# The end of layer 1 of a two-layer recurrent backbone: head 5's output products behind head 7's gates, heads 6 and 7 summed in PSUM, the last norm's squares summed by TensorE

## The chip, the core and the metric

The kernel runs on one core of a Trainium2 chip. The core has TensorE (PE in the profile), which multiplies matrices into PSUM; VectorE (DVE), ScalarE (ACT) and GpSimd (POOL), which work elementwise; and SyncE (SP), which here issues most of the transfers from HBM. Each engine takes its instructions from a queue in the order in which the program was built, and waits in that order. The metric is the time of one execution in microseconds (us), the median of several runs.

## The reference, cut to what matters

A sequence of 256 context tokens and 512 latent tokens (a grid of 8 x 64), 1024 channels wide, goes through two layers. Layer 0 is a gated linear recurrence with 16 heads and is not touched by the change. Layer 1 is this, for each of its 8 heads of 256 channels (all in float32):

```python
xb, g = split(h @ w_in)                      # h: normed and modulated tokens
xb = conv_centred(xb, conv_w, conv_b)        # width 4
r  = sigmoid(xb @ w_a[d] + b_a[d])           # d: two directions
ig = sigmoid(xb @ w_x[d] + b_x[d])
a  = exp(-8 * r * softplus(-lam[d]))
u  = sqrt(1 - a * a) * (ig * xb)
y  = scan(a, u, d=0) + scan(a, u, d=1)       # h[t] = a[t] * h[t-1] + u[t]
x  = x + gate * ((y * silu(g)) @ w_out)      # summed over the heads
out = x * rsqrt(mean(x * x) + eps) * final_norm_g
```

Only the 512 latent tokens are put out.

## The kernel before

**Layout.** Channels lie on the 128 partitions, tokens along the free axis. Each head of layer 1 has two chunks of 128 channels, called `jc`, `e` or `u` (0 and 1). The output has 8 chunks of 128 channels, called `d`. Every product is exact to float32: each operand is split into a high and a low float32r part, and `mm3` issues three matmuls per pair (lines 308, 309, 310: high x high, high x low, low x high).

**Weights.** They come as a stream of [128, 1024] tiles (class `Weights`). Each is loaded by SP into a `raw` tile (line 114); ScalarE copies out the high part `hi` (line 129), VectorE subtracts to get `lo` (line 130). There are three buffers each for `raw`, `hi` and `lo`, so a tile's split waits until the tile three places earlier in the stream has been used up by TensorE.

**A head of layer 1** consists of these parts, named as in the profile:

- `rin`: products of the normed tokens, `r` (PSUM, pool `dps`, four buffers). `x = 0` gives `xb` by the convolution (ScalarE line 758, VectorE line 761), then its two parts `xh` (763) and `xl` (764). `x = 1` gives the output gate `gg` (a sigmoid on ScalarE, line 742, and a product on VectorE, 743).
- `mixer`: the gates. For each of the four keys (direction, chunk), 24 matmuls of 384 columns into four `gt` tiles (PSUM, pool `aps`, four buffers), which ScalarE turns into `R` and `G` by sigmoids (809), and VectorE multiplies `G` by `xb` (811). Then ScalarE takes tanh (818) and two exponentials (820, 821) of each key, then the square roots of all keys (827). VectorE makes `T` (822), the driven input (830), the scans (832 forward; 835 and 836 backward), sum and gate (839, 840); ScalarE and VectorE split the result into `yh` (841) and `yl` (842). Sigmoid, exp and sqrt lie in different function tables of ScalarE, so that each change of kind has an ACT_TABLE_LOAD.
- `rout`: the head's output, 48 matmuls of 512 columns into eight `ro` tiles (`dps`), each added to the residual stream by VectorE (`add_out`, line 848).

`R`, `G` and `T` have four buffers each: a sigmoid of head j + 1 waits until VectorE has scanned the same key of head j.

**Order.** The main loop over the heads runs the mixer as a generator and lets other work be issued between its steps (`interleave`, `phase`): during the gates of head j and during the functions behind them, the products `rin` of head j + 1 and `rout` of head j - 1. For head 6 (`elif not last`) half of head 7's `rin` stands in the first phase and `rout` of head 5 in the second. For head 7 (`else`) the first three keys' gates run with the output-gate half of its own `rin`, the fourth key is a group of its own behind them, and nothing else is between. The program is then scheduled by a framework, which fixes the order on each engine at build time; priorities (`high_priority`, `issue_after`) bend it.

**The end.** `rout(6)` runs whole. Then the products of head 7 with its chunk 0, for all eight `d` over 512 tokens: five are held in PSUM, three are added to the residual at once. Then, for each half of 256 tokens, the products with chunk 1, `add_out`, and `sumsq`: ScalarE squares a chunk (lines 282, 285), and GpSimd and VectorE add the squares into three accumulators (286). `rstd_of` sums the accumulators over the partitions by matmuls of one column (`msf`, line 259), takes the root on ScalarE (262) and its reciprocal (263), and spreads it by `rbf` (269). Sixteen VectorE operations (922) and eight transfers put out the result.

Of the kernel before, what the change touches and what calls it, by code (L numbers as in the profile page):

```python
# [16 lines left out]
NT = CTX + LAT          # tokens, context first  # L17
HN = NT // 2            # token half
ROWS, GW = 8, 64        # latent grid
DK = 8                  # 128-channel chunks of the model width  # L20
NH = 16                 # HGRN2 heads
NC = NT // P            # chunks of 128 tokens
NLEV = 7                # block sizes 1, 2, ... 64 within a chunk
NM = 5                  # of these, the ones within 32 tokens
RH = 8                  # RG-LRU heads
EPS = 1e-6

# the order of the start: a step of adaLN block b (ab), the norm (r), chunk k of h (hk), the weights of the first head's
# product y (wy), their part with chunk k of h (fky), the split of the first value weights (v)
# [3 lines left out]
# columns of the packed parameters  # L33
# [7 lines left out]
# columns of the constants: identity, row selector, 1/1024, 1/128  # L41
# [10 lines left out]
def perm(ap):  # L52
    """latent columns in column-major grid order, walked row by row"""
    return ap.rearrange("p (w r) -> p r w", r=ROWS)
# [6 lines left out]
def phase(main, weight, filler, total):  # L61
    """interleave up to the next None of main, if weight is that of one phase"""
    interleave(upto(main, weight), weight, filler, total)
# [12 lines left out]
class Nothing:  # L76
    """stands in for the program while the order of the weight tiles is taken down"""
# [16 lines left out]
class Weights:  # L94
    """the stream of [128, 1024] weight tiles, loaded ahead and split into two float32r parts"""
# [60 lines left out]
def interleave(main, weight, filler, total):  # L156
    """after each step of main (yields give its weight), its share of the filler (yields give its size)"""
# [11 lines left out]
def build(tc, ins, out, plan):  # L169
# [19 lines left out]
    # ---- constants, small parameters, the residual stream  # L189
# [24 lines left out]
    # silu of both condition vectors, padded to 32 columns  # L214
# [7 lines left out]
    # ---- adaLN: six blocks of 512 columns, four parts of the contraction side by side in the array  # L222
# [28 lines left out]
    # ---- h = rms(x) * g * (1 + scale) + shift, as two float32r parts  # L251
    def rstd_of(accs, ones, tag, parts, between=()):
        """1 / sqrt(mean + eps) of each token from its squares (chunks of 128 tokens; the mean is over the partitions
        and accs), on all partitions: PSUM tiles of so many chunks"""
# [23 lines left out]
    def sumsq(accs, groups, tile_, k, c):  # L278
        """the squares of chunk k of the channels, summed by groups of chunks; the first of three groups on GpSimd"""
# [13 lines left out]
    def hchunk(l, k, i, rs, scr):  # L293
        """chunk k of h for one stretch of tokens; layer 0 keeps the latents in row-major order"""
# [9 lines left out]
    def mm3(ps, pairs, first=True, last=True, skip=False):  # L304
        """exact products of split operands: ps += sum over (whi, wlo, xhi, xlo) of whi xhi + whi xlo + wlo xhi"""
# [9 lines left out]
    # ================= layer 0  # L315
# [98 lines left out]
    def prep(h):  # L414
        """operands of the first two score steps"""
# [9 lines left out]
    def hgrn(h):  # L425
# [4 lines left out]
        # scores [key, query]: same token (both directions), then pairs of neighbouring blocks of 1, 2, ... 64 tokens;  # L430
        # up to 32 tokens the array works on four groups of 32 keys at once
# [49 lines left out]
        # keys with tokens on the partitions (in place), for the chunk states  # L481
# [7 lines left out]
        # states that enter the chunks, in the order of each direction  # L489
# [237 lines left out]
    turn = {}  # L727

    def after(*names):
        """queue ScalarE's instructions behind the last ones of these kinds"""  # L730
        stack = ExitStack()
        for n in names:
            if n in turn:
# [268 lines left out]
```

## Time and profile before

| | |
|---|---|
| median of 3 runs | 1648.79 us (1645.66 to 1650.98) |
| span of the profiled execution, first to last instruction | 1643.9 us |
| median less span, taken as what lies around the span | 4.9 us |
| last stage: first gates of head 6 to the end | 1520.2 to 1643.9 us |
| longest idle time of TensorE after the start | 8.8 us, at 1604.4 |
| busy share over the span | PE 97%, DVE 73%, ACT 52%, POOL 1% |

The page shows the busy share of each engine. A timeline row has the start in the span, the duration, engine, line, operation, what is written and read, how many like instructions were merged, and in brackets how long the engine was idle before it and what ended that. Instructions of one engine overlap a little: on ScalarE the next one starts about 0.1 us before the shown end of the former. Shown ends of matmuls are modelled, so their cost is the distance of their starts.

### The profile page before, as it was taken

How to read it: one execution, taken by the hardware profiler on the slowest of the kernel's cores; microseconds unless marked ns; L12 is line 12 of the kernel's file. 1: busy time of each engine (PE TensorE's matmuls, PEld its weight loads, DVE VectorE, ACT ScalarE, POOL GpSimd, SP SyncE). 2: the span in 40 equal slices, each digit the busy share in tenths (PEclk: the TensorE clock that was granted, in tenths of full speed). 3: DMA queues.
4: the chain of work that ended last, by engine and by line, in shares of the span. 5: the costliest groups of instructions: out<-in, count | busy, mean ns of one | idle time of the engine just before them, and what ended most of it. 6: DMA issues, size and time to landing. Idle time of an engine off the chain costs nothing.

```text
span 1643.9 us, 33639 instructions
## 1 busy us (share of the span) xinstructions
PE 1595.2 (97%) x14548; PEld 1432.9 (87%) x14548; DVE 1203.1 (73%) x1867; ACT 856.0 (52%) x1359; POOL 11.8 (1%) x16
## 2 busy tenths in 40 slices
PE   6999999999999999999999999999999999999995
PEld 3888899999999999898989889888798888888884
DVE  5756668767867777756866675787758977887888
ACT  5544354444443453443444344544567677577774
POOL 0000000000000000000000000001000000000001
PEclk9999999999999999999999999999899999999997
DMA  8222211110211211213031222211022222222211
GB/s 340 65 78 65 91 53 47 58 53 27 75 43 40 66 53 40 82 61 97 33 117 48 82 78 65 89 42 40 26 91 76 74 68 77 74 68 64 78 64 51
DMA packets 33858, 116.76 MB, mean 71 GB/s; under 512 B 3632, under 2 KB 6064, under 8 KB 33712
## 3 DMA queue, kind: packets, MB, share of 16 engines
q1 hardware_dynamic: 32192, 113.26, 21.7%
q8 instruction: 114, 1.87, 0.5%
q10 hardware_dynamic: 1520, 1.37, 0.3%
q14 instruction: 32, 0.26, 0.0%
HBM read 112.52 MB, written 2.10 MB: 70 GB/s over the span
## 4 chain that ended last, share of the span: by engine, by line
PE 88%; DVE 7%; ACT 2%; issue 1%; DMA 1%; POOL 0%; ACTq 0%; POOLq 0%; DVEq 0%
PE in L308 12%; PE in L309 11%; PE in L310 11%; PE v L378 8%; PE ada L228 4%; PE lv L456 4%; PE o L531 3%; PE r L310 3%; PE r L308 3%; PE r L309 3%; PE o L308 3%; PE o L309 3%; PE o L310 2%; PE U L499 2%; PE gt L308 2%; PE gt L309 2%
## 5 line engine op out<-in xcount | busy, mean ns | idle before, releaser
L308 PE MATMUL in<-h_hi,hi 128*128 128x384 f32 x1024 | 355.1, 348 | 1.6 <-ACT h_hi L301 1.6
L309 PE MATMUL in<-h_lo,hi 128*128 128x384 f32 x1024 | 344.7, 337 | 0.4 <-DVE h_lo L302 0.4
L310 PE MATMUL in<-h_hi,lo 128*128 128x384 f32 x1024 | 344.4, 337 | 0.0
L129 ACT ACTIVATE hi<-raw 128x1024 fp32r<-128x1024 f32 x160 | 168.4, 1057 | 195.8 <-PE in L309 106.6
L130 DVE TENSOR_TENSOR lo<-raw,hi 128x1024 fp32r<-128x1024 f32 x160 | 195.0, 1220 | 92.9 <-ACT hi L129 92.8
L308 PEld LDWEIGHTS in<-h_hi,hi 128*128 128x128 f32 x1024 | 192.1, 188 | 35.9 <-issue 27.7
L309 PEld LDWEIGHTS in<-h_lo,hi 128*128 128x128 f32 x1024 | 192.6, 188 | 2.4 <-issue 1.7
L310 PEld LDWEIGHTS in<-h_hi,lo 128*128 128x128 f32 x1024 | 192.3, 188 | 1.7 <-DVE amul L246 0.8
L466 DVE TENSOR_TENSOR QQ<-QQ,T 128x768 f32<-128x768 f32 x112 | 117.4, 1048 | 94.1 <-PE lv L456 94.1
L412 ACT ACTIVATE kt<-KK 128x768 f32<-128x768 f32 x112 | 102.1, 912 | 52.9 <-DVE KK L459 50.0
L310 PE MATMUL r<-h_hi,lo 128*128 128x512 f32 (+1 forms) x344 | 123.7, 360 | 3.7 <-DVE lo L130 3.7
L334 ACT ACTIVATE sg<-in 128x384 f32<-128x384 f32 x128 | 61.9, 485 | 125.2 <-PE in L310 125.1
L459 DVE TENSOR_TENSOR KK<-KK,T 128x768 f32<-128x768 f32 x112 | 117.0, 1045 | 11.7 <-ACT kt L412 11.7
L309 PE MATMUL r<-h_lo,hi 128*128 128x512 f32 (+1 forms) x344 | 123.1, 358 | 0.0
L308 PE MATMUL r<-h_hi,hi 128*128 128x512 f32 (+1 forms) x344 | 123.0, 358 | 0.0
L378 PE MATMUL v<-hi,h_hi 128*128 128x256 f32 x384 | 111.9, 291 | 0.0
L378 PE MATMUL v<-lo,h_hi 128*128 128x256 f32 x384 | 107.5, 280 | 0.0
L378 PE MATMUL v<-hi,h_lo 128*128 128x256 f32 x384 | 107.4, 280 | 0.0
L228 PE MATMUL ada<-raw,sc 128*32 128x512 f32 x192 | 81.2, 604 | 14.2 <-DMA raw<-in_ada_dram 14.2
L554 DVE RECIPROCAL sq<-sq 128x384 f32<-128x384 f32 x30 | 75.9, 2541 | 21.3 <-ACT sq L548 21.2
L402 DVE SCALAR_TENSOR_TENSOR x<-o,ada,x 128x256 f32<-128x256 f32 (+1 forms) x184 | 82.2, 490 | 12.6 <-PE o L310 12.2
L308 PE MATMUL o<-rhi,hi 128*128 128x384 f32 (+2 forms) x240 | 86.2, 361 | 2.2 <-DVE lo L130 1.2
(202 smaller groups left out, 3286.2 us busy)
## 6 DMA issues: line engine op xcount, KB each, us to landing
raw<-in_hgw_dram SPq DMA_DIRECT2D x64, 512.0 KB, 3.5
raw<-in_ada_dram SPq DMA_DIRECT2D x48, 512.0 KB, 3.7
raw<-in_rgi_dram SPq DMA_DIRECT2D x32, 512.0 KB, 3.8
raw<-in_hgv_dram SPq DMA_DIRECT2D x16, 512.0 KB, 3.4
raw<-in_hgo_dram SPq DMA_DIRECT2D x16, 512.0 KB, 3.5
raw<-in_rgg_dram SPq DMA_DIRECT2D x16, 512.0 KB, 3.5
raw<-in_rgo_dram SPq DMA_DIRECT2D x16, 512.0 KB, 3.8
x<-in_x_dram SPq DMA_DIRECT2D x8, 384.0 KB, 6.0
```

The lines of the kernel that those rows point to most:

```text
L129: self.nc.scalar.activation(hi, r, AF.Copy)
L130: self.nc.vector.tensor_tensor(lo, r, hi.bitcast(F32), ALU.subtract)
L228: PE.matmul(ps[32 * j:32 * j + 32, :], lhsT=sc[:, 2 * j + k, :], rhs=w[:, 512 * k:512 * k + 512], start=k == 0, stop=k == 1, tile_position ...
L308: PE.matmul(ps, lhsT=wh, rhs=xh, start=first and i == 0, stop=False, skip_group_check=skip)
L309: PE.matmul(ps, lhsT=wh, rhs=xl, start=False, stop=False, skip_group_check=skip)
L310: PE.matmul(ps, lhsT=wl, rhs=xh, start=False, stop=last and i == n - 1, skip_group_check=skip)
L378: PE.matmul(ps, lhsT=xh[:, kk, t], rhs=w[:, k], start=part == 0 and k == 0 and i == 0 and c % 2 == 0, stop=part == 1 and k == 3 and i == 2 ...
L402: V.scalar_tensor_tensor(xs, ps[:, a - c.start:b - c.start], gate[:, d, 1 - j:2 - j], xs, ALU.mult, ALU.add)
L412: A.activation(view(kt, 0, [[2 * B, n], [B, 2], [1, B]]), view(KK, 0, [[2 * B, n], [NT + B, 2], [1, B]]), AF.Copy)
L459: V.tensor_tensor(kv, kv, view(T, 1, [[2, n], [m - 1, 2], [0, B]]), ALU.mult)
L466: V.tensor_tensor(qv, qv, view(T, m + 1, [[2, n], [-m - 1, 2], [0, B]]), ALU.mult)
L554: V.reciprocal(rs, rs)
```

## The change

The change does five things.

1. Head 6's mixer now has head 7's whole `rin` beside it: the convolution half (`ALL[2:]`) in the first phase with a weight that spreads it over all the gates, the output-gate half (`ALL[:2]`) in the second phase. Before, the second phase held `rout(5)`, and the output-gate half lay beside head 7's gates.
2. Head 7's first group of gates runs with nothing beside it in the source; `rout(5)` is interleaved with all that follows it.
3. Heads 6 and 7 share their PSUM tiles: for six of the eight `d` the 48 products of head 6 and those of head 7 add up in the same tile, and only the sum goes to the residual. For `d` = 6 and 7 head 6 is added by itself, and head 7's products come into a shared tile `pt` by halves of 256 tokens.
4. The squares of the eight chunks are no longer added on GpSimd and VectorE; each stays in its own place, and the one-column matmuls sum all eight: 16 such matmuls for a half of the tokens in place of 6.
5. `yp` has three buffers in place of two. The space for DMA programs that GpSimd would write is set to 1024 bytes.

```diff
-    xbp, xrp, ggp, yp = p1("xbp", 2), p1("xrp"), p1("ggp", 2), p1("yp", 2)
+    xbp, xrp, ggp, yp = p1("xbp", 2), p1("xrp"), p1("ggp", 2), p1("yp", 3)
...
         elif not last:
-            phase(m, 8.0, rin(j + 1, ALL[2:]), 5000.0)
-            phase(m, 20.0, rout(j - 1), 10400.0)
+            phase(m, 8.0, rin(j + 1, ALL[2:]), 15600.0)
+            phase(m, 20.0, rin(j + 1, ALL[:2]), 10400.0)
         else:
-            phase(m, 6.0, rin(j, ALL[:2]), 10400.0)
-            run_all(m)
-
-    run_all(rout(RH - 2, 0))
-    j = RH - 1
...
-    accs2 = [cp.tile([P, NT], F32, name=f"acc2{i}", tag="R") for i in range(3)]
-    ws = [wget("rout", 2 * j + e) for e in range(2)]
+            run_all(upto(m, 6.0))
+            interleave((w for w in m if w is not None), 22.0, rout(j - 2), 10400.0)
...
+    j, HELD = RH - 1, 6
+    ws = [wget("rout", 2 * j - 2 + e) for e in range(2)]
     pss = []
     for d in range(DK):
-        ps = (dtile if d < 4 else atile)(f"ro{j}_{d}")
-        mm3(ps, part(d, (0,), slice(0, LAT)), last=d >= 5, skip=True)
-        if d < 5:
+        ps = (dtile if d < 4 else atile)(f"ro{j - 1}_{d}")
+        mm3(ps, part(j - 1, d, (0, 1), slice(0, LAT)), last=d >= HELD, skip=True)
+        if d < HELD:
             pss.append(ps)
         else:
             add_out(ps, d, 0)
+    ws = [wget("rout", 2 * j + e) for e in range(2)]
+    for d in range(HELD):
+        mm3(pss[d], part(j, d, (0,), slice(0, LAT)), first=False, last=False, skip=True)
...
-        for d in range(DK):
-            ps = pss[d][:, c] if d < 5 else (dtile if i else atile)(f"ro{j}_{d}_{i}")[:, :H]
-            mm3(ps, part(d, (1,), c), first=d >= 5, last=d >= 5 or i == 1, skip=True)
+        pt = atile(f"ro{j}_{HELD}_{i}")
+        for d in (*range(HELD, DK), *range(HELD)):
+            ps = pss[d][:, c] if d < HELD else pt[:, H * (d - HELD):H * (d - HELD) + H]
+            mm3(ps, part(j, d, (1,) if d < HELD else (0, 1), c), first=d >= HELD, last=d >= HELD or i == 1, skip=True)
             add_out(ps, d, 0, cx)
-            sumsq(accs2, THREE, lambda n: cp.tile([P, NT], F32, name=n, tag="G"), d, cx)
-            if i == 1 and d == 4:
-                stats(0)
-    stats(1)
+            n = len(sqs[i])
+            if n % 3 == 0:
+                sq = cp.tile([P, NT], F32, name=f"sq{i}_{n}", tag="RG"[i])
+            t = sq[:, H * (n % 3):H * (n % 3) + H]
+            A.activation(t, x1[:, d, cx], AF.Square)
+            sqs[i].append(t)
+            if i == 1 and d == 1:
+                rsf.extend(rstd_of([chunks(a, slice(0, H)) for a in sqs[0]], ones_d, "f0", (2,)))
+    rsf.extend(rstd_of([chunks(a, slice(0, H)) for a in sqs[1]], ones_d, "f1", (2,)))
...
-    nc = _bacc.Bacc("TRN2", target_bir_lowering=False, num_devices=1)
+    nc = _bacc.Bacc("TRN2", target_bir_lowering=False, num_devices=1, dynamic_dma_scratch_size=1024)
```

The instructions stand so on the engines. In the names a letter group is followed by the head: `T6_0_1` is tile T of head 6, direction 0, chunk 1; `gg7` is head 7's output gate, `hi204` the high part of the 204th weight tile (204 and 205 are head 6's output weights, 206 and 207 head 7's).

ScalarE between the exponentials of head 6 and the first sigmoid of head 7, before:

```order
L820 ACTIVATE A6_0_1_16238<-R6_0_1_16030,spc_576 128x768
L818 ACTIVATE T6_1_1_16081<-R6_1_1_16079,spc_576 128x768
L821 ACTIVATE R6_0_1_16030<-R6_0_1_16030,spc_576 128x768
L820 ACTIVATE A6_1_1_16251<-R6_1_1_16079,spc_576 128x768
L763 ACTIVATE xh7_16001<-xb7_16000 128x768
L821 ACTIVATE R6_1_1_16079<-R6_1_1_16079,spc_576 128x768
L827 ACT_TABLE_LOAD
```

and now:

```order
L820 ACTIVATE A6_0_1_16229<-R6_0_1_16061,spc_576 128x768
L742 ACT_TABLE_LOAD
L742 ACTIVATE gg7_16245<-r7_1_0_1_16210 128x512
L821 ACT_TABLE_LOAD
L821 ACTIVATE R6_0_1_16061<-R6_0_1_16061,spc_576 128x768
L818 ACTIVATE T6_1_1_16147<-R6_1_1_16145,spc_576 128x768
L820 ACTIVATE A6_1_1_16249<-R6_1_1_16145,spc_576 128x768
L129 ACTIVATE hi202_16390<-raw202_16310 128x1024
L821 ACTIVATE R6_1_1_16145<-R6_1_1_16145,spc_576 128x768
L827 ACT_TABLE_LOAD
```

A sigmoid of head 7's output gate now stands among the exponentials, with a table load on either side of it; the convolution's instructions have left this place.

ScalarE at the square roots of head 7's first three keys, before:

```order
L827 ACT_TABLE_LOAD
L827 ACTIVATE T7_0_0_16327<-T7_0_0_16327 128x768
L827 ACTIVATE T7_1_0_16397<-T7_1_0_16397 128x768
L827 ACTIVATE T7_0_1_16458<-T7_0_1_16458 128x768
L809 ACT_TABLE_LOAD
L809 ACTIVATE R7_1_1_16535<-gt7_1_1_0_0_16538,prm_76 128x384
```

and now:

```order
L827 ACT_TABLE_LOAD
L827 ACTIVATE T7_0_0_16318<-T7_0_0_16318 128x768
L129 ACTIVATE hi204_16443<-raw204_16435 128x1024
L129 ACTIVATE hi205_16586<-raw205_16441 128x1024
L129 ACTIVATE hi206_16592<-raw206_16584 128x1024
L827 ACTIVATE T7_1_0_16354<-T7_1_0_16354 128x768
L827 ACTIVATE T7_0_1_16396<-T7_0_1_16396 128x768
L809 ACT_TABLE_LOAD
L809 ACTIVATE R7_1_1_16519<-gt7_1_1_0_0_16522,prm_76 128x384
```

Three splits of weight tiles now stand between the roots; before, one of them (`hi206`) stood a little earlier, among the exponentials, and two were done before the exponentials.

VectorE ahead of the last key's scans, before:

```order
L842 TENSOR_TENSOR yl7_16318<-T7_1_0_16397,yh7_16317 128x512
L848 SCALAR_TENSOR_TENSOR x1_81<-ro6_6_16644,ada1_97,x1_81 128x512
L848 SCALAR_TENSOR_TENSOR x1_81<-ro6_7_16652,ada1_97,x1_81 128x512
L830 TENSOR_TENSOR G7_1_1_16536<-G7_1_1_16536,T7_1_1_16537 128x768
L835 SCALAR_TENSOR_TENSOR T7_1_1_16537<-R7_1_1_16535,G7_1_1_16536 128x256
```

and now:

```order
L840 TENSOR_TENSOR T7_1_0_16354<-T7_1_0_16354,gg7_16245 128x512
L130 TENSOR_TENSOR lo207_16655<-raw207_16590,hi207_16654 128x1024
L848 SCALAR_TENSOR_TENSOR x1_81<-ro6_6_16638,ada1_97,x1_81 128x512
L848 SCALAR_TENSOR_TENSOR x1_81<-ro6_7_16646,ada1_97,x1_81 128x512
L842 TENSOR_TENSOR yl7_16309<-T7_1_0_16354,yh7_16308 128x512
L830 TENSOR_TENSOR G7_1_1_16520<-G7_1_1_16520,T7_1_1_16521 128x768
L835 SCALAR_TENSOR_TENSOR T7_1_1_16521<-R7_1_1_16519,G7_1_1_16520 128x256
```

The low part of the last weight tile (`lo207`) has moved in between chunk 0's gate (line 840) and the last key's product (line 830). `hi207`, which it needs, now stands on ScalarE between the last exponential and the last root; before, it stood between the first two sigmoids of the last key.

## Rows read from the trace of the kernel before

**Rows 1.** The page, first part: busy time, share and instructions of each engine

```profile
PE 1595.2 (97%) x14548; PEld 1432.9 (87%) x14548; DVE 1203.1 (73%) x1867; ACT 856.0 (52%) x1359; POOL 11.8 (1%) x16
```

**Rows 2.** Timeline of TensorE: head 7's `rin` behind head 6's gates; the hole

```profile
1543.24 0.39 PE L308 MATMUL r<-h_hi,hi 128*128 128x512 f32 x1
...
1554.46 0.40 PE L308 MATMUL ro<-yh,hi 128*128 128x512 f32 x1
...
1613.16 1.22 PE L308 MATMUL ro<-yh,hi 128*128 128x512 f32 x2 [8.79 <-ACT yh L841]
```

**Rows 3.** Busy time in stretches of 2 us around the hole; PEclk is granted clock

```profile
1608.00:1610.00 2.00, 0.00 (x0) 0.00 (x0) 2.00 (x3) 2.00 (x3) 0.00 (x0) 0.50 0.00 0
...
1616.00:1618.00 2.00, 2.00 (x7) 1.55 (x6) 1.90 (x4) 0.10 (x1) 0.00 (x0) 0.52 0.00 0
```

**Rows 4.** Timeline of ScalarE, heads 6 and 7

```profile
1544.74 0.93 ACT L818 ACTIVATE T<-R,spc 128x768 f32<-128x768 f32 x1
...
1574.38 1.05 ACT L809 ACTIVATE R<-gt,prm 128x384 f32<-128x384 f32 x2
...
1586.74 0.64 ACT L841 ACTIVATE yh<-T 128x512 fp32r<-128x512 f32 x1 [2.76 <-DVE T L840]
...
1590.09 0.96 ACT L818 ACTIVATE T<-R,spc 128x768 f32<-128x768 f32 x1
...
1605.10 0.58 ACT L809 ACTIVATE R<-gt,prm 128x384 f32<-128x384 f32 x1
...
1612.48 0.63 ACT L841 ACTIVATE yh<-T 128x512 fp32r<-128x512 f32 x1 [1.38 <-DVE T L840]
...
1615.25 0.85 ACT L827 ACTIVATE T<-T 128x768 f32<-128x768 f32 x1
...
1620.68 0.63 ACT L841 ACTIVATE yh<-T 128x512 fp32r<-128x512 f32 x1 [4.58 <-DVE T L840]
```

**Rows 5.** ScalarE's groups from 1544.7 to 1574.4: count, busy, mean ns, idle before

```profile
L129 ACT ACTIVATE hi<-raw 128x1024 fp32r<-128x1024 f32 x4 | 4.1, 1052 | 0.4 <-PE ro L309 0.4
...
L827 ACT ACTIVATE T<-T 128x768 f32<-128x768 f32 x4 | 3.3, 838 | 2.3 <-DVE T L822 2.3
L763 ACT ACTIVATE xh<-xb 128x768 fp32r<-128x768 f32 x2 | 1.7, 838 | 0.0
L758 ACT ACTIVATE xb<-r,prm 128x512 f32<-128x512 f32 x2 | 1.5, 766 | 0.0
...
L809 ACT ACT_TABLE_LOAD x1 | 1.3, 1283 | 2.6 <-DVE T L832 2.6
...
L758 ACT ACTIVATE xb<-r,prm 128x256 f32<-128x256 f32 x1 | 0.6, 554 | 0.0
```

**Rows 6.** Timeline of VectorE, head 6's scans to the end

```profile
1569.52 1.82 DVE L830 TENSOR_TENSOR G<-G,T 128x768 f32<-128x768 f32 x2
...
1579.26 1.22 DVE L130 TENSOR_TENSOR lo<-raw,hi 128x1024 fp32r<-128x1024 f32 x1
...
1614.70 1.41 DVE L848 SCALAR_TENSOR_TENSOR x<-ro,ada,x 128x512 f32<-128x512 f32 x2
1616.13 0.96 DVE L830 TENSOR_TENSOR G<-G,T 128x768 f32<-128x768 f32 x1
...
1621.83 0.68 DVE L842 TENSOR_TENSOR yl<-T,yh 128x512 fp32r<-128x512 f32 x1
...
1638.94 1.65 DVE L922 SCALAR_TENSOR_TENSOR fin_xl<-x,prm,rbf 128x256 f32<-128x256 f32 x4
```

**Rows 7.** Timeline of TensorE in the last norm (each `msf` matmul leaves two records)

```profile
1628.10 0.28 PE L310 MATMUL ro<-yh,lo 128*128 128x256 f32 x1
1628.22 0.95 PE L259 MATMUL msf<-cst,acc 128*128 128x1 f32 x8
1629.03 0.36 PE L308 MATMUL ro<-yh,hi 128*128 128x256 f32 x1
...
1632.30 2.72 PE L259 MATMUL msf<-cst,acc 128*128 128x1 f32 x12 [1.86 <-POOL acc L286]
```

More of the change, by code (lines that the diff above doesn't have):

```diff
@@ L871, in build, with part @@
         elif not last:
-            phase(m, 8.0, rin(j + 1, ALL[2:]), 5000.0)
-            phase(m, 20.0, rout(j - 1), 10400.0)
-        else:
-            phase(m, 6.0, rin(j, ALL[:2]), 10400.0)
-            run_all(m)
-    run_all(rout(RH - 2, 0))
-    j = RH - 1
-    s = rt[j]
-    accs2 = [cp.tile([P, NT], F32, name=f"acc2{i}", tag="R") for i in range(3)]
-    ws = [wget("rout", 2 * j + e) for e in range(2)]
-    def part(d, us, c):
+            phase(m, 8.0, rin(j + 1, ALL[2:]), 15600.0)
+            phase(m, 20.0, rin(j + 1, ALL[:2]), 10400.0)
+        else:
+            run_all(upto(m, 6.0))
+            interleave((w for w in m if w is not None), 22.0, rout(j - 2), 10400.0)
+    def part(j, d, us, c):
         e = slice(P * d, P * d + P)
-        return [(ws[u][0][:, e], ws[u][1][:, e], s["yh"][:, u, c], s["yl"][:, u, c]) for u in us]
+        return [(ws[u][0][:, e], ws[u][1][:, e], rt[j]["yh"][:, u, c], rt[j]["yl"][:, u, c]) for u in us]
+    j, HELD = RH - 1, 6
+    ws = [wget("rout", 2 * j - 2 + e) for e in range(2)]
     pss = []
     for d in range(DK):
-        ps = (dtile if d < 4 else atile)(f"ro{j}_{d}")
-        mm3(ps, part(d, (0,), slice(0, LAT)), last=d >= 5, skip=True)
-        if d < 5:
+        ps = (dtile if d < 4 else atile)(f"ro{j - 1}_{d}")
+        mm3(ps, part(j - 1, d, (0, 1), slice(0, LAT)), last=d >= HELD, skip=True)
+        if d < HELD:
             pss.append(ps)
@@ L900, in build @@
            enumerate((((xbp, "xb"), (xbp, "xb")), ((xrp, "xh"), (xrp, "xl"))))]
-    def stats(i):
-        cx = slice(CTX + H * i, CTX + H * i + H)
-        rsf.extend(rstd_of([chunks(a, cx) for a in accs2], ones_d, f"f{i}", (2,)))
+    sqs = [[], []]
     for i in range(2):
```

## The prediction, made before the changed kernel was run

> **What bounds the kernel now.** I read the page first: TensorE is busy 97% of the span [rows 1], so work moved about can only pay where TensorE waits. Its timeline has one large wait: at 1613.2 it has stood idle for 8.8 us, until ScalarE delivers head 7's first `yh` (line 841) [rows 2]. The stretches around it show the second cost of the hole: the granted clock is 0.50, the level of 1.2 GHz, when the matmuls return, and is back at 2.4 GHz just before 1618 [rows 3]. I then asked what the `yh` waits for. On ScalarE's timeline the `yh` shown are themselves late because of VectorE's line 840, by 2.8, 1.4 and 4.6 us [rows 4]. So the end is set by a chain that goes to and fro between ScalarE and VectorE: sigmoids, exponentials and roots of head 6, its scans, the sigmoids of head 7 (which need the buffers those scans release), and so on to head 7's last `yh` at 1620.68. TensorE only keeps pace with it. I therefore follow that chain through the change, station by station, on the clock of the profiled execution. Its span is 1643.9 us; the median of the runs is 4.9 us above, and I add that at the end.
>
> **The change part by part.**
>
> *Head 7's `rin` beside head 6's gates.* Before, 11.2 us of `rin` (1543.24 to 1554.46) lay behind head 6's last gate [rows 2]; they now lie ahead of it, so the last gate, and with it the chain, comes 11.2 us later, at 1554.5. In front of its last sigmoid ScalarE now also has a split and an `xh`. With overlaps of 0.1 us taken off, these cost 0.95 and 0.74, and the sigmoid 0.47 [rows 4, 5]. Tanh begins at about 1556.8, against 1544.74.
>
> From that tanh to head 7's first sigmoid ScalarE took 29.6 us (to 1574.38) [rows 4], of which it waited 2.3, 2.6 and 0.4 [rows 5]: 24.3 of work. Three convolution starts (1.8 together), one `xh` (0.74) and two splits (1.9) are gone [rows 5]: 19.9. Added are two output-gate sigmoids, priced as the 512-column `yh` at 0.54 each [rows 4], and, as one of them stands among the exponentials, two more table loads of 1.28 [rows 5]: 23.6. The waits for VectorE I take as gone, since head 5's eight `add_out` (0.66 each [rows 6]) and the convolution no longer stand in its queue there. Head 7's first sigmoid comes at 1580.4, 6.0 us late. Its bounds: if both loads fell into a wait that remains, 2.6 less; if the old waits stay, 5.3 more. Meanwhile TensorE has only 11.2 us of output-gate products and one key's gates under it, and will stand idle for several us.
>
> A table load in the rows is 1283 ns, with no idle time in the group beside it [rows 5]. The Trainium skill (ScalarE: Activation LUTs, section What ACT_TABLE_LOAD costs) counts a drain of some 1.4 us with every switch, and its rule is to batch by table set, which this order breaks. By that figure the two loads would cost 2.8 us more and the sum below would be 1658.5; I go by the row.
>
> *Head 7's gates.* The first root of head 6 begins 4.8 us ahead of 1580.4 (four roots of 0.75, a load, a sigmoid), so VectorE starts its products at 1576.4. Before, it needed 17.2 us from there (1569.52) to head 6's second `yh` (1586.74) [rows 4, 6], with two `lo` in between (the first one is shown; 1.1 each) [rows 6] that now stand elsewhere: 15.0, to 1591.4. Behind that `yh` (0.54) stand three sigmoids (1.4): head 7's tanh at 1593.3, against 1590.09. So 2.8 us of the delay is won back here, because the output-gate products no longer lie between the gates.
>
> *The functions of head 7's first three keys.* 15.0 us before, 1590.09 to 1605.10 [rows 4], with one split among them. Now there are three, 1.9 us more: 1610.2, 5.1 late. At the other end the extra splits would be hidden only if ScalarE waited here, and the rows show no wait; so 0 to 1.9.
>
> *The last key.* From its first sigmoid to its root 10.15 us (1605.10 to 1615.25) [rows 4]. Chunk 0's `yh` stood in between, with a wait of 1.4; it now stands behind the root, which takes out 1.9. In its place the root waits for VectorE's line 822, which is behind the three `lo` of the splits; I allow 0.8, about one operation (bounds 0 and 3.4, three `lo`). And the last split waits for TensorE to have used head 6's weights up, which I take as about in time. 9.1: the root at 1619.3, 4.0 late.
>
> From the root to the last `yh` it was 5.4 us, and VectorE took up the root's result at once (line 830 at 1616.13) [rows 6]. Now `lo207` (1.1), two `add_out` (1.3) and a `yl` (0.6) stand in front [rows 6], 3.0 in all, of which I let 0.4 pass under the root. The last `yh` comes at 1627.3, 6.6 us later than before. TensorE's hole does shrink, since head 5's products fill it, but it breaks up: waits near 1570, 1576 and 1616 take the place of one.
>
> *PSUM sum of heads 6 and 7.* The matmul columns are the same. VectorE loses nine `add_out` of 512 columns, 5.9 us. Six of them lay at 1596 to 1602 beside ScalarE's exponentials, where nobody waited for them; the others come back as 256-column ones or lay between the scans' end and the tail. Worth nothing on the path.
>
> *Squares by TensorE.* Gone are 4 adds on VectorE, 6 on GpSimd, and the wait of 1.86 for GpSimd [rows 7]. Added are 20 one-column matmuls, 32 in place of 12. Eight records took 0.81 us from start to start at the full clock, so 0.2 us for a matmul; twelve took 2.72 at the half clock, 0.45 [rows 7]. After the last `yh` TensorE now has 54 matmuls of 256 columns at 0.12 (6.5), 32 at 0.2 (6.4), two spreads (0.6) and a wait for `yl` (0.7) [rows 6, 7]: 14.2 us to the end of the sums. Before it was 14.3 (1620.68 to 1635.02). So the adds' saving is spent on TensorE, which now sets the tail. Behind it the reciprocal has 14 final products in place of 13 (0.4 each [rows 6]). The tail was 23.2 us (to 1643.9) and becomes 23.5.
>
> *The rest.* The weight loads change order, not number; no wait in the rows above names a transfer. The third `yp` buffer and the DMA space move no instruction. Nothing.
>
> **Sum.** 1627.3 + 23.5 = 1650.8 for the span, 6.9 over before. With 4.9: 1655.7.
>
> **The rivals.**
>
> *TensorE sets the end, and the hole is filled.* 39 of head 5's 48 products, for which the source counts 10.4 us, are 8.5 us, and the hole is 8.8 [rows 2]. If the chain were no later than before, that gain would be whole: 1648.8 - 8.5 = 1640.3. For it: the 97%. Against: the hole's releaser is ScalarE, and ScalarE's and VectorE's work gets no earlier start. It decides if head 7's first sigmoid comes by about 1575.
>
> *The two halves keep pace.* If ScalarE's waits elsewhere swallow the three splits (1.9) and VectorE's queue ahead of the last scans is empty by the root (2.6 and 0.8), the chain loses 1.6 us only: 1650.4, which is no change.
>
> *The half clock in the tail.* The waits that the change leaves for TensorE near 1570, 1576 and 1616 are 3 to 5 us each; rows 3 show the level of 1.2 GHz after a hole of 8.8, and no wait here between 2 and 8 us tells which way one of 4 falls. In that case head 7's chunk 0 products (18 of 512 columns and 12 of 256, 5.8 us at 0.12 for 256 columns [rows 7], for which about 6 are at hand) overrun by 1 to 2; and the last sixteen `msf`, if the clock is low there as it was before, take 7.2 in place of 3.2. Together about 5: 1660.5. The Trainium skill (TensorE: Matmul & The Clock Gate, section HAM oscillation) warns that bursts of matmuls with waits between them fall back to the half clock again and again; rows 3 agree for the long hole, nothing here shows it for the short ones.
>
> *No change in order.* The scheduler might have undone the source's order; the rows of the order above show that it has not. No chance given.
>
> **How the numbers follow.** What a measurement can tell from no change is about 0.3%, 4.9 us, so 1643.9 to 1653.7 is "the same". Forecast 0.60, with its own range 1652.5 to 1658.5; filled hole 0.12; kept pace 0.16; half clock 0.12. Slower is most of the forecast (0.55) and the half clock: 0.67. The same is the pace and the rest of the forecast: 0.21. Faster is the filled hole: 0.12. The range reaches down to 1649 into the kept pace and up to 1661; what is left out is the filled hole and a little of each side.
>
> **What would show it.** Right: ScalarE's first sigmoid of head 7 near 1580 with two table loads more before it; waits of 3 to 5 us on TensorE for ScalarE's line 809 and its splits; the last `yh` near 1627; the tail bound by `msf` on TensorE. Wrong: that sigmoid before 1576, or a TensorE that runs without a wait into head 7's `ro`; a tail under 21 us from the last `yh`; or VectorE taking up line 830 as soon as the last root is done.

## The result: 0.5% slower, through the chain and a tail that hangs on the clock

The changed kernel took 1656.62 us in the median (1654.77 to 1661.44, 5 runs), the kernel before 1648.79 (1645.66 to 1650.98, 5 runs). The ratio is 1.0053, 95% interval 1.0035 to 1.0072: slower, by 7.8 us in the medians. The forecast was 1655.7.

**A mark to count from.** Two executions of one kernel differ by some us before the change is even reached, so stations are compared from a mark ahead of it: the table load for head 5's last sigmoids. ScalarE's timeline of the kernel before (columns: start, duration, engine, line, operation, out<-in, shapes, count, [idle before, what ended it]):

```profile
65.19 1.28 ACT L334 ACT_TABLE_LOAD   x1
...
1467.68 1.28 ACT L809 ACT_TABLE_LOAD   x1 [2.96 <-DVE T L832]
```

and of the changed kernel:

```profile
1468.48 1.28 ACT L809 ACT_TABLE_LOAD   x1 [2.96 <-DVE T L832]
...
1557.50 0.93 ACT L818 ACTIVATE T<-R,spc 128x768 f32<-128x768 f32 x1
...
1567.34 1.28 ACT L742 ACT_TABLE_LOAD   x1
1568.63 0.60 ACT L742 ACTIVATE gg<-r 128x512 f32<-128x512 f32 x1
1569.25 1.28 ACT L821 ACT_TABLE_LOAD   x1
...
1576.20 3.04 ACT L827 ACTIVATE T<-T 128x768 f32<-128x768 f32 x4
...
1581.05 1.05 ACT L809 ACTIVATE R<-gt,prm 128x384 f32<-128x384 f32 x2
...
1592.29 0.63 ACT L841 ACTIVATE yh<-T 128x512 fp32r<-128x512 f32 x1 [1.69 <-DVE T L840]
...
1594.21 0.94 ACT L818 ACTIVATE T<-R,spc 128x768 f32<-128x768 f32 x1
...
1605.39 2.94 ACT L129 ACTIVATE hi<-raw 128x1024 fp32r<-128x1024 f32 x3
...
1611.11 1.05 ACT L809 ACTIVATE R<-gt,prm 128x384 f32<-128x384 f32 x2
...
1619.85 0.84 ACT L827 ACTIVATE T<-T 128x768 f32<-128x768 f32 x1 [0.46 <-DVE T L822]
...
1627.94 0.63 ACT L841 ACTIVATE yh<-T 128x512 fp32r<-128x512 f32 x1 [6.72 <-DVE T L840]
```

These rows answer to [rows 4, 5]. The changed trace is 0.80 late at the mark; that is taken off every station below:

| station, us after the mark | before | predicted delay | changed | delay |
|---|---|---|---|---|
| tanh of head 6 | 77.06 | 12.1 | 89.02 | 11.96 |
| first sigmoid of head 7 | 106.70 | 6.0 | 112.57 | 5.87 |
| tanh of head 7 | 122.41 | 3.2 | 125.73 | 3.32 |
| first sigmoid of the last key | 137.42 | 5.1 | 142.63 | 5.21 |
| last root | 147.57 | 4.0 | 151.37 | 3.80 |
| last `yh` | 153.00 | 6.6 | 159.46 | 6.46 |
| end of the span | 176.22 | 6.9 | 184.52 | 8.30 |

The reader sees the `gg` sigmoid between two table loads, the four roots without the wait for VectorE that they had, and the three splits (`hi`) between roots. From the last `yh` to the end it was 23.2 us and is 25.1. VectorE's timeline shows why `yh` comes 8.1 us after the root in place of 5.4:

```profile
1620.34 1.21 DVE L130 TENSOR_TENSOR lo<-raw,hi 128x1024 fp32r<-128x1024 f32 x1
1621.48 1.40 DVE L848 SCALAR_TENSOR_TENSOR x<-ro,ada,x 128x512 f32<-128x512 f32 x2
1622.80 0.68 DVE L842 TENSOR_TENSOR yl<-T,yh 128x512 fp32r<-128x512 f32 x1
1623.40 0.95 DVE L830 TENSOR_TENSOR G<-G,T 128x768 f32<-128x768 f32 x1
```

The root was done near 1620.7; line 830 begins 2.7 us later, behind a `lo`, two `add_out` and a `yl`. In [rows 6] it followed within 0.1 us.

TensorE is still 97% busy, and POOL has lost the six adds of the last norm (page, first part):

```profile
PE 1605.3 (97%) x14594; PEld 1439.2 (87%) x14594; DVE 1195.7 (72%) x1854; ACT 859.5 (52%) x1361; POOL 7.0 (0%) x10
```

The hole of 8.79 us [rows 2] has become three waits, and the tail ends on the one-column matmuls (TensorE's timeline):

```profile
1574.13 0.79 PE L308 MATMUL ro<-yh,hi 128*128 128x512 f32 x1 [3.27 <-ACT hi L129]
1581.68 0.69 PE L308 MATMUL gt<-xh,hi 128*128 128x384 f32 x1 [2.94 <-ACT R L809]
...
1621.27 1.87 PE L308 MATMUL ro<-yh,hi 128*128 128x512 f32 x4 [3.39 <-ACT yh L841]
...
1628.62 0.98 PE L308 MATMUL ro<-yh,hi 128*128 128x256 f32 x6 [0.24 <-ACT yh L841]
...
1633.16 2.74 PE L259 MATMUL msf<-cst,sq 128*128 128x1 f32 x24
...
1639.32 4.35 PE L259 MATMUL msf<-cst,sq 128*128 128x1 f32 x32
1644.22 1.22 PE L269 MATMUL rbf<-cst,rf 128*128 128x128 f32 x4 [0.55 <-DVE rf L263]
```

Busy time in stretches (columns: stretch, its length, busy time of PE, PEld, DVE, ACT, POOL with counts, granted clock, DMA share, GB/s):

```profile
1573.70:1587.20 13.50, 10.09 (x26) 8.18 (x27) 11.75 (x13) 10.36 (x15) 0.00 (x0) 0.50 0.12 40
...
1621.40:1624.70 3.30, 2.90 (x7) 1.81 (x8) 3.27 (x6) 0.00 (x0) 0.00 (x0) 0.52 0.00 0
1624.70:1641.80 17.10, 16.86 (x132) 16.02 (x131) 11.13 (x24) 7.04 (x18) 0.00 (x0) 0.99 0.00 1
1641.80:1644.30 2.50, 1.95 (x12) 1.86 (x11) 0.30 (x2) 0.26 (x1) 0.00 (x0) 0.54 0.31 105
```

The clock is at 1.2 GHz (0.50) after the waits of 3.27 and 3.39, and again from 1642.0, while TensorE is in the middle of the last `msf`.

### The profile page after: what moved, and what is told of

Read it like the earlier page. It is cut to its first block, busy times and chain, and to the rows that moved or that the text cites. A ratio compares the mean times of both kernels' runs of the same rounds, so it can differ in the third digit from the quotient of the medians.

```text
span 1653.0 us, 33695 instructions
## 1 busy us (share of the span) xinstructions
PE 1605.3 (97%) x14594; PEld 1439.2 (87%) x14594; DVE 1195.7 (72%) x1854; ACT 859.5 (52%) x1361; POOL 7.0 (0%) x10
## 4 chain that ended last, share of the span: by engine, by line
PE 85%; DVE 8%; ACT 4%; issue 1%; DMA 1%; POOL 0%; ACTq 0%; DVEq 0%
PE in L308 12%; PE in L309 11%; PE in L310 11%; PE v L378 8%; PE ada L228 4%; PE lv L456 4%; PE o L531 3%; PE r L310 3%; PE r L308 3%; PE r L309 3%; PE o L308 3%; PE o L309 2%; PE o L310 2%; PE U L499 2%; DVE lo L130 2%; PE gt L308 2%
## 5 line engine op out<-in xcount | busy, mean ns | idle before, releaser
L308 PE MATMUL gt<-xh,hi 128*128 128x384 f32 x256 | 86.8, 342 | 3.4 <-ACT R L809 2.9
```

What stands on the lines that cost most here:

```text
L308: PE.matmul(ps, lhsT=wh, rhs=xh, start=first and i == 0, stop=False, skip_group_check=skip)
```

## The experiments

Twelve runs followed (e10 is the changed kernel again), each beside runs of the kernel before on the same chip. Tails and stations come from one profiled execution of each. The table gives the median, the ratio with its interval, and from the profiled execution the last `yh` and the end of the span after the mark, and the tail between them.

| kernel | median | ratio to before | last `yh` | tail | end |
|---|---|---|---|---|---|
| before | | | 153.00 | 23.2 | 176.2 |
| changed | 1656.6 | 1.0053 [1.0035, 1.0072] | 159.46 | 25.1 | 184.5 |
| e1 | 1652.5 | 1.0021 [1.0011, 1.0030] | 152.38 | 26.6 | 179.0 |
| e2 | 1654.4 | 1.0036 [1.0026, 1.0047] | 153.81 | 30.1 | 183.9 |
| e3 | 1656.8 | 1.0045 [1.0030, 1.0060] | 157.19 | 27.2 | 184.3 |
| e4 | 1657.2 | 1.0047 [1.0032, 1.0062] | 159.51 | 22.6 | 182.1 |
| e5 | 1651.1 | 1.0016 [1.0001, 1.0032] | 152.99 | 23.8 | 176.8 |
| e6 | 1655.0 | 1.0035 [1.0023, 1.0047] | 157.11 | 27.1 | 184.2 |
| e7 | 1656.1 | 1.0043 [1.0030, 1.0057] | 159.45 | 24.6 | 184.0 |
| e8 | 1641.9 | 0.9953 [0.9941, 0.9964] | 146.04 | 24.4 | 170.4 |
| e9 | 1648.8 | 0.9996 [0.9988, 1.0005] | 152.37 | 24.4 | 176.8 |
| e10 | 1657.1 | 1.0055 [1.0039, 1.0071] | 159.47 | 30.1 | 189.5 |
| e11 | 1651.7 | 1.0013 [1.0005, 1.0022] | 153.81 | 24.5 | 178.3 |
| e12 | 1643.7 | 0.9970 [0.9958, 0.9981] | 146.05 | 27.3 | 173.3 |

The theory was the chain of the prediction; its rivals that TensorE sets the end, and that the half clock does.

**e1: head 7's inputs behind head 6's last gate again.**

```
-            phase(m, 8.0, rin(j + 1, ALL[2:]), 15600.0)
+            phase(m, 8.0, rin(j + 1, ALL[2:]), 5000.0)
```

> The changed kernel with one number put back: head 7's first input products again mostly behind head 6's last gate (5000 in place of 15600 at line 872); head 5's output products stay behind head 7's gates, the PSUM sum and the squares by TensorE stay. Chain theory (the 11.2 us of products ahead of head 6's last gate are the loss; where head 5's products stand is of no matter): head 6's first tanh back at 1545 +- 1, last yh at 1620 to 1621.5, 1648 to 1651 us, so 6 to 8 below the changed kernel and level with the one before. Rival, TensorE sets the end and its hole is now filled: 1640 to 1642. Rival, the loss comes from moving head 5's products (their adds and splits in front of the last scans): stays at 1654 to 1657.

ScalarE's timeline of e1: the mark, head 6's tanh, a table load of the `gg` sigmoid, the three splits, the last `yh`:

```profile
1471.91 1.28 ACT L809 ACT_TABLE_LOAD   x1 [2.96 <-DVE T L832]
...
1548.98 0.93 ACT L818 ACTIVATE T<-R,spc 128x768 f32<-128x768 f32 x1
...
1565.35 1.28 ACT L742 ACT_TABLE_LOAD   x1
...
1602.02 2.94 ACT L129 ACTIVATE hi<-raw 128x1024 fp32r<-128x1024 f32 x3
...
1624.29 0.63 ACT L841 ACTIVATE yh<-T 128x512 fp32r<-128x512 f32 x1 [6.60 <-DVE T L840]
```

Tanh is back at 77.07 after the mark and the last `yh` at 152.38, 7.1 earlier than in the changed kernel and 0.6 earlier than before, with head 5's products still late. So the chain's loss hangs on this one number, though the other costs are still there: the two table loads stand among the exponentials, the three splits between the roots, and the last `yh` comes 8.0 after the root. Head 7's tanh is 4.9 earlier than before (117.5 after the mark, against 122.4), and that pays for them. The filled hole of the rival (1640) didn't come. But the time fell by 4.1 us only, to 1652.5, above the 1648 to 1651 expected: the tail is 26.6.

**e2: the old order of the phases, with PSUM sum and squares by TensorE.**

```
-            phase(m, 8.0, rin(j + 1, ALL[2:]), 15600.0)
-            phase(m, 20.0, rin(j + 1, ALL[:2]), 10400.0)
+            phase(m, 8.0, rin(j + 1, ALL[2:]), 5000.0)
+            phase(m, 20.0, rout(j - 1), 10400.0)
         else:
-            run_all(upto(m, 6.0))
-            interleave((w for w in m if w is not None), 22.0, rout(j - 2), 10400.0)
+            phase(m, 6.0, rin(j, ALL[:2]), 10400.0)
+            run_all(m)
```

> The changed kernel with the order of the phases of heads 6 and 7 as it was before; the sum of heads 6 and 7 in PSUM and the squares by TensorE stay. Chain theory: these two parts are worth -1 to +2 us at the end, so 1648 to 1651 us, last yh at 1620.5 to 1622, 23.5 to 25 us from there to the end of the span. Rival, the PSUM sum and the tail carry most of the loss: 1653 to 1657 with the last yh at 1621.

1654.4, above the 1651 of the theory and within the 1653 to 1657 of its rival: with the order as before, these two parts alone cost 6.3 us against the kernel before (1648.1 on that chip). The last `yh` was where it was expected, 0.8 later than before; the tail was not, 30.1 us. Its stretches:

```profile
1621.30:1628.30 7.00, 6.34 (x30) 6.34 (x31) 3.97 (x9) 3.40 (x8) 0.00 (x0) 0.52 0.00 0
1628.30:1631.50 3.20, 3.20 (x31) 3.20 (x29) 1.50 (x4) 0.94 (x3) 0.00 (x0) 1.00 0.00 0
1631.50:1638.20 6.70, 6.70 (x33) 6.70 (x33) 1.82 (x5) 2.11 (x7) 0.00 (x0) 0.50 0.00 0
1638.20:1642.00 3.80, 3.80 (x34) 3.77 (x33) 1.26 (x3) 0.77 (x2) 0.00 (x0) 0.95 0.22 73
```

Two stretches at 0.50: one after a wait of 3.3 us for the last `yh`, and one of 6.7 in which TensorE was busy without a gap, behind most of the first 24 one-column records (they begin at 1629.04). The chain alone doesn't give the tail; the half clock is in it.

**e3: without head 5's output products.** The products, their eight adds and the splits of two weight tiles are left out of the result.

```
-            interleave((w for w in m if w is not None), 22.0, rout(j - 2), 10400.0)
+            run_all(m)
```

> Leaves out part of the result: head 5's 48 output products, their eight adds and the split of their two weight tiles. Chain theory: 11 us of TensorE work less beside head 7's gates and functions move the end only by what ScalarE and VectorE lose with them (two splits and eight adds, of which part lies in waits): last yh 1.5 to 3.5 us earlier, 1653 to 1655 us, TensorE's waits before the last yh longer by about 8. Rival, TensorE sets the end: 1645 to 1647, 10 to 11 below the changed kernel.

TensorE's waits in e3, which answer to the three above:

```profile
1585.43 0.69 PE L308 MATMUL gt<-xh,hi 128*128 128x384 f32 x1 [10.81 <-ACT R L809]
...
1613.58 0.79 PE L308 MATMUL ro<-yh,hi 128*128 128x512 f32 x1 [7.49 <-ACT R L809]
...
1630.03 1.43 PE L308 MATMUL ro<-yh,hi 128*128 128x256 f32 x6 [3.62 <-ACT yh L841]
```

48 products less, and the time is 1656.8, as with them and above the 1653 to 1655 expected: these three waits are 21.9 us together, against 9.6 in the changed kernel, so the time of the products turned into waits for ScalarE. The last `yh` came 2.3 us earlier, as expected of the missing splits and adds; the tail of 27.2 took it back. That TensorE sets the end ahead of the tail is refuted.

**e4: squares by adds on VectorE and GpSimd.**

```
-            A.activation(t, x1[:, d, cx], AF.Square)
-            sqs[i].append(t)
+            sumsq(accs2, ((6, 1, 4), (7, 2, 5), (0, 3)), lambda n: cp.tile([P, NT], F32, name=n, tag="G"), d, cx)
```

> The changed kernel with the squares of the last norm summed as before, by adds on VectorE and GpSimd, and 12 one-column matmuls in place of 32; all else as changed. Theory (the 20 more matmuls took what the adds gave back, and at the half clock at the end a little more): the last yh stays at 1628 +- 0.5; from there to the end of the span 23 to 24.5 in place of 25.1, so 1654.5 to 1656.5 us. Rival, the tail is paced by VectorE's adds into the residual and by ScalarE's squares: 25 to 26.5 from the last yh, 1656.5 to 1658.

In the profiled execution the last `yh` is where it was and the tail 22.6 us, 2.5 shorter, with a time of 1652.97. The other four runs took 1656.65 to 1657.8, so the median, 1657.2, shows no gain and lies above the 1654.5 to 1656.5 expected. What those four spent isn't in any trace; this run alone would not decide it.

**e5: the kernel before with the squares by TensorE alone.**

```
-            sumsq(accs2, THREE, lambda n: cp.tile([P, NT], F32, name=n, tag="G"), d, cx)
+            A.activation(t, x1[:, d, cx], AF.Square)
+            sqs[i].append(t)
```

> The kernel before with one part of the change alone: the squares of the last norm summed by 32 one-column matmuls in place of 12 and the adds. The order of the heads is the old one, so the last yh must stay at 1620.7 (counted from the table load near 1524.5: +96.2). Theory now (the one-column matmuls are long, and the granted clock falls to 0.5 during or just after them): from the last yh to the end of the span 25 to 30 us in place of 23.2, so 1650 to 1655. Rival, the tail is VectorE's and ScalarE's, and the matmuls lie under it: 22.5 to 23.5, 1647 to 1649. If the 30 us of the old order with the PSUM sum came from the PSUM sum (48 matmuls behind the last yh), this kernel shows 24 or less.

Tail 23.8, below the 25 to 30 of the theory and within the "24 or less" of the other reading. In the profiled execution the clock was 1.00 from the last `yh` through nearly all of the sums, with most of the 64 one-column records among them:

```profile
1622.80:1636.90 14.10, 14.02 (x119) 13.60 (x117) 9.79 (x23) 6.55 (x18) 0.00 (x0) 1.00 0.06 20
```

So these matmuls aren't always followed by the half clock. The median, within the theory's 1650 to 1655, is 2.3 us above before and the runs lie 10 us apart (1646.21 to 1656.44; before 1644.88 to 1650.84).

**e6: head 7's output-gate sigmoid out of the exponentials.**

```
-            phase(m, 20.0, rin(j + 1, ALL[:2]), 10400.0)
+            phase(m, 20.0, rin(j + 1, ALL[:2]), 5200.0)
```

> The changed kernel with head 7's first output-gate product a little later (5200 in place of 10400 at line 873), so that its sigmoid stands behind head 6's roots with the other sigmoids and not among the exponentials: two table loads of 1.28 fewer. Chain theory: head 7's first sigmoid 2.5 to 3.5 earlier against head 6's tanh, the last yh 2 to 2.5 earlier (117.6 to 118.3 from that tanh's head 5 mark becomes 119.5 at most, against 121.7), and 2 us off the time: 1653.5 to 1655.5, if the tail stays at 25 to 27. Rival, the loads lie in waits that remain: no change in the last yh.

Two table loads fewer, and the last `yh` 2.35 us earlier, within 2 to 2.5. Of that 1.7 shows in the median, 1655.0, with a tail of 27.1 in the profile; the interval overlaps that of the changed kernel, so the gain is shown on the chain and not in the time.

**e7: one wide matmul a square.**

```
+            PE.matmul(pm, lhsT=ones_d.to_broadcast([P, P]), rhs=a, start=n == 0, stop=n == DK - 1)
```

> The changed kernel with each 256-token square summed by one matmul against a 128x128 block of 1/1024 in place of two one-column ones; the sums come out on all partitions, so the reciprocal is wide (128x256, on VectorE) and the four spreading matmuls go. If the one-column form is what lowers the clock (few columns while the engine counts as busy): the granted clock stays at 1.0 from the last yh until the last of these matmuls, and the tail is 22.5 to 25. Rival, the clock falls in the tail because of the hole ahead of the last yh: it is at 0.5 in the same places, 25 to 28. The wide reciprocal costs 0.3 to 1.7 us that the narrow one did not.

The clock held from the last `yh` to the end of the sums:

```profile
1631.20:1646.10 14.90, 14.64 (x94) 13.16 (x93) 10.35 (x23) 7.65 (x19) 0.00 (x0) 1.00 0.00 0
```

But the form costs what it saves. TensorE's and then VectorE's timeline of e7:

```profile
1642.20 3.64 PE L907 MATMUL msw<-sq,cst 128*128 128x256 f32 x16
```

```profile
1646.45 1.74 DVE L910 RECIPROCAL rw<-rw 128x256 f32<-128x256 f32 x1
```

Eight wide matmuls (16 records) took 3.64 us, and each wide reciprocal 1.74 where the narrow one took 0.17, so the tail is 24.6 and the time that of the changed kernel. This is one profile, and in e5 the clock held with one-column matmuls too; that the form lowers the clock isn't shown.

**e8: a version by the chain theory.** Head 4's products go beside head 6's functions, head 5's beside head 7's, so that head 6's gates come earlier; PSUM sum as in the change, squares by adds.

```
+        elif j == RH - 3:
+            phase(m, 8.0, rin(j + 1, ALL[:2]), 10400.0)
+            phase(m, 20.0, rin(j + 1, ALL[2:]), 15600.0)
         elif not last:
             phase(m, 8.0, rin(j + 1, ALL[2:]), 5000.0)
+            phase(m, 20.0, rout(j - 2), 10400.0)
         else:
+            phase(m, 6.0, rin(j, ALL[:2]), 10400.0)
```

> Towards a faster kernel, by the chain theory: head 4's output products move beside head 6's functions and head 5's beside head 7's functions, so that head 6's last gate comes about 7 us earlier (tanh at 1537.5 in place of 1544.7); head 7's first input products start behind head 6's gates as before (5000), its output-gate products beside its own gates as before; PSUM sum of heads 6 and 7 as in the change, squares by adds as before. Chain theory: last yh 6.5 to 7.5 us earlier than before (1613 to 1614), tail 22.5 to 25, so 1640 to 1645 us. Rival, TensorE's 97% bounds it or the third yp buffer and the weights hold it up: 1647 or more.

ScalarE's timeline of e8:

```profile
70.31 1.28 ACT L334 ACT_TABLE_LOAD   x1
...
1472.37 1.28 ACT L809 ACT_TABLE_LOAD   x1 [2.96 <-DVE T L832]
...
1542.20 0.96 ACT L818 ACTIVATE T<-R,spc 128x768 f32<-128x768 f32 x1
...
1618.41 0.63 ACT L841 ACTIVATE yh<-T 128x512 fp32r<-128x512 f32 x1 [5.31 <-DVE T L840]
```

Head 6's tanh comes 7.2 us earlier than before (69.83 after the mark), the last `yh` 7.0, and the time is 1641.9, ratio 0.9953: 0.5% faster than before, as the theory had it (1640 to 1645). The PSUM sum, which costs 2.1 us by itself (e11), is still in it.

**e9: the edits of e1 and e4 together.**

> Two edits of earlier runs together: head 7's first input products again behind head 6's last gate, and the squares by adds. If the loss is the sum of the two (chain 7.1 and squares 2.4 in the profiles): last yh 152.4 after ScalarE's table load for head 5's sigmoids (before: 153.0), tail 22.5 to 23.5, end of the span 175 to 176 after that load (before: 176.2), so 1646.5 to 1649, level with the kernel before. Rival, a hole of TensorE just ahead of the tail keeps the clock at 0.5 in it whatever sums the squares: tail 25 to 27, 1650 to 1653.

1648.8, ratio 0.9996: the two edits bring the kernel back level with before, with head 5's products late, the PSUM sum, the third `yp` buffer and the new order of the weight loads all still in it, though the tail of 24.4 is 1 us over the range expected (the clock was 0.51 from 1615.2 to 1621.6, around the last `yh`).

**e10: the changed kernel again,** with no edit.

> The changed kernel itself, for a second profile. Up to the last yh it must repeat to 0.2 us, counted from the table load for head 5's sigmoids (+159.5). If the tail's length hangs on where the granted clock falls and not on the order of the instructions, it differs from 25.1 by more than 0.5 (23.5 to 29); if the tail is set by the instructions alone it is 24.9 to 25.3.

```profile
1628.55 0.88 PE L308 MATMUL ro<-yh,hi 128*128 128x256 f32 x6
...
1640.20 6.82 PE L259 MATMUL msf<-cst,sq 128*128 128x1 f32 x32
1647.57 1.22 PE L269 MATMUL rbf<-cst,rf 128*128 128x128 f32 x4 [0.55 <-DVE rf L263]
```

The same instructions, the last `yh` at 159.47 as in the first profile, and a tail of 30.1 in place of 25.1. The last 32 records took 6.82 us against 4.35, and they begin 13.95 us after the last `yh` against 11.38: the first products that need this `yh` start 2.3 us behind it and not 0.7, because TensorE is late with the ones ahead of them. The stretches of e10 show why.

```profile
1621.50:1627.80 6.30, 5.95 (x14) 4.70 (x15) 5.21 (x7) 0.63 (x1) 0.00 (x0) 0.51 0.00 0
1627.80:1638.10 10.30, 10.30 (x88) 10.20 (x87) 4.57 (x12) 4.29 (x12) 0.00 (x0) 0.99 0.00 0
1638.10:1647.50 9.40, 8.92 (x43) 8.83 (x42) 3.08 (x9) 2.40 (x7) 0.00 (x0) 0.50 0.09 30
```

So one order of instructions gives two tails, 5.0 us apart, and they differ in where the clock is low: in e10 until 1627.6 and again from 1637.9.

**e11: the PSUM sum alone.** The edit of e2 on top of that of e4, which leaves only this part of the change.

> The kernel before with one part of the change alone: the outputs of heads 6 and 7 summed in PSUM (squares by adds, order of the phases as before). Last yh +153.8 as with both parts (head 5's mark as above). If the 30.1 us of tail seen with both parts came from TensorE's wait of 3.3 us just ahead of the last yh, at whose end the clock was 0.5: the tail is 25 to 28 here too and the time 1650 to 1654. Rival, it came from the one-column matmuls: 22.5 to 23.5 and 1647 to 1650.

The last `yh` 0.8 later, as the last weight tile's low part (1.2 us on VectorE) now stands between line 830 and the scan, and the tail 24.5, with the clock at 0.53 for 3 us behind a wait of 3.24: 2.1 us in the medians, between the two expectations (the time as the first, the tail just short of it). VectorE's timeline of e11:

```profile
1619.74 0.96 DVE L830 TENSOR_TENSOR G<-G,T 128x768 f32<-128x768 f32 x1 [0.89 <-ACT T L827]
1620.69 1.22 DVE L130 TENSOR_TENSOR lo<-raw,hi 128x1024 fp32r<-128x1024 f32 x1
1621.84 0.68 DVE L835 TENSOR_TENSOR_SCAN T<-R,G 128x256 f32<-128x256 f32 x1
```

**e12: e8 with the squares by TensorE,** so without e4's edit.

> The faster order of the earlier run (head 4's and 5's output products each a head later) with the squares by TensorE as in the change in place of the adds. Last yh unchanged, +146.0. If the one-column matmuls are what lengthens the tail: 25 to 30 us in place of 24.4, so 1642.5 to 1647. Rival, they are free where the order is better: 24.4 or less, 1640 to 1642.

The last `yh` as in e8, the tail 27.3, the time 1643.7, 1.8 above e8.

## Why the prediction was right, and which term was off

**The chain.** Each station came within 0.2 us of the predicted delay, the last `yh` at +6.46 against +6.6, and so did the stretch with the most terms in it: from head 6's tanh to head 7's first sigmoid 23.55 us, against 23.6. That the 11.2 us of `rin` ahead of head 6's last gate start it is shown by e1, which takes back only these. The 7.1 it gives back is less than the 12 by which head 6's tanh moves, since the work that had gone ahead of that tanh lies behind it again: from there to head 7's first sigmoid e1 takes 29.3 us, the changed kernel 23.6. That TensorE merely keeps pace is shown by e3 and e1.

**The table loads.** Priced at two of 1.28; e6, without them, was 2.35 earlier. The Trainium skill (ScalarE: Activation LUTs, What ACT_TABLE_LOAD costs) counts a drain with each switch, some 5.3 us for two by its total. Here ScalarE's next operation begins 0.01 us after the load (1567.34 and 1568.63), and e6 gained no more than the loads.

**The last key.** The root's allowance for VectorE was 0.8 and measured 0.46; the queue in front of line 830 was taken as 2.6 and measured 2.7.

**The tail, the mis-sized term.** "The tail was 23.2 us (to 1643.9) and becomes 23.5": it was 25.1 in one profile of the same kernel and 30.1 in the other. That the adds' saving would be spent on TensorE was right in direction. The size was wrong because everything behind the last `yh` was priced at the full clock. In the first profile the last sixteen `msf` took 4.35 in place of 3.2. The rival of the half clock had both other prices: 7.2 us for these sixteen, and e10 shows 6.82; 1 to 2 us of overrun for chunk 0's products, and e10 shows 1.6 (2.3 less 0.7). The PSUM sum and the squares, priced at 0.3 together, cost 6.3 us with the old order (e2). With the squares by TensorE the tail was 23.8 to 30.1 in eight profiles (mean 27.2); with adds 22.6 to 24.5 in five (mean 23.8). Five pairs ran both ways in one order. In four the adds have the lower median: e9 by 3.7 against e1, e11 by 2.7 against e2, before by 2.3 against e5, e8 by 1.8 against e12. In the fifth, e4 against the changed kernel, they don't (1657.2 and 1656.6), and why stays open; most pairs ran on different chips, and as ratios to the kernel before beside them all five are lower with the adds, the fifth by less than its interval (1.0047, against 1.0053 and 1.0055). The half clock, given 0.12 as a rival, is thus a part of what happened rather than a case beside it.

**The PSUM sum, "worth nothing on the path".** Alone it cost 2.1 us (e11): 0.8 ahead of the last `yh`, where the low part of the last weight tile has moved into VectorE's last scans, and 1.3 in the tail. There TensorE waits 3.24 us for the last `yh`, and the clock behind that wait is 0.53; before, it had products left there and didn't wait. That the wait causes the 1.3 fits these rows, but no run has the PSUM sum in this order without it.

**What lies around the span.** I added 4.9, the median less the span. In every run whose span is on record the time lies only 1.7 to 2.2 above that execution's own span (1654.77 and 1653.0 for the changed kernel), and 1643.9 plus 2 is near the fastest run of before, 1645.66. So about 3 us of the 4.9 were the distance from the profiled execution to the median one. Executions part by as much in their start, but one profile of before can't show that it was this. For the changed kernel the median is 3.6 above the profiled span, so this term was 1.3 too large, while the span of 1650.8 was 2.2 too small (1653.0: 1.6 from the tail, 0.8 from ahead of the mark, 0.1 back from the chain). That the forecast of 1655.7 missed by 0.9 only is in part luck: the two errors offset each other.

**The rivals.** The filled hole is refuted (e1, e3). The kept pace is too: ScalarE had no wait that could swallow the three splits, and the last key's first sigmoid came 5.2 late. TensorE's waits foreseen near 1570, 1576 and 1616 begin at 1570.9, 1578.7 and 1617.9. The half clock holds for the tail, and its 1660.5 lies within the runs of the changed kernel (1654.8 to 1663.3), though well above their median.

## What to carry to other kernels

A 97% busy engine can still be the follower: find the station where it waits, ask what released it, and leave out its work (e3) before moving it. Products that nothing waits for yet belong behind the gate that starts the critical chain, not ahead of it: with the output products of heads 4 and 5 each moved a head later, and head 7's inputs left where they were, the kernel gained 0.5% (e8) where the change lost 0.5%. In the last stretch, count the waits after which TensorE comes back at half the clock, price the one-column matmuls at both levels, and take more than one profile before pricing the stretch.

## What the runs showed of the hardware

- **The clock falls without a wait.** In e2 TensorE was busy for all of 6.70 us at 0.50, and the fall came among the first one-column matmuls; in e10 the clock fell at 1637.9, behind 10.3 us without a gap. With wide matmuls in their place (e7) it held 1.00 for 14.9 us, but so it did for 14.1 us with one-column ones in e5. What makes it fall isn't shown. The Trainium skill (TensorE: Matmul & The Clock Gate, HAM oscillation) speaks of waits between bursts, and the waits of 3.2 to 3.5 us here agree (0.50 to 0.53 behind them in the changed kernel, e2, e8, e10 and e11). In e1 a wait of 3.44 was followed by 1.00, in e9 with the same order up to there by 0.51. What decides between those isn't in the rows.
- **Where executions part.** Between 14 us and 65 us of the start, e8 fell 5.0 us behind before (70.31 against 65.19); from there to 1085 us the two stay together to 0.1 us. One more step, of up to 0.8, lies between 1126 and 1188 us. From the mark on, everything up to the last `yh` repeats to some 0.1 us.
- **Thin reciprocals are cheap, wide ones not.** 128x2 took 0.17 us, 128x256 took 1.74, against 0.48 for a multiply-add of that size.
